# A two-block transformer kernel: projections tied to scores, value halves side by side, differential output by query blocks without normalising, and scaling and gate products on ScalarE and GpSimd

## The chip, the cores and the metric

One core of a Trainium2 chip. TensorE (PE in the profile) multiplies, VectorE (DVE) and ScalarE (ACT) do elementwise work and empty PSUM, GpSimd (POOL) does elementwise work from SBUF, and SyncE (SP) and ScalarE issue DMAs. Each engine runs its own instructions in order. The metric is the device time of the one launch, in microseconds (us).

## The reference

512 tokens of width 1024, float32, pass through two blocks. Cut to what bears on the change:

```python
# block 1
h = rms_norm(x) * (1 + scale) + shift          # shift, scale, gate = silu(c) @ w_ada + b_ada
oa = forgetting_attention(qa, ka, va, fa)      # 8 heads of 64, causal: softmax(qk/8 + c_q - c_k) @ v
ob = sliding_window_sink_attention(qb, kb, vb) # 8 heads of 64 on 2 key heads, window 128, with a sink
y = concat(oa * silu(za), ob * silu(zb)) @ w_out
x = x + gate * rms_norm(y)
# block 2: h @ w_in feeds a convolution, a differential attention and a cross attention
p = softmax(q k / 8 + alibi, causal)           # 8 heads, 2 maps each, q and k normalised
o = (p[0] - lam * p[1]) @ v                    # 128 columns a head
o = rms_norm(o) * subln * 0.8 * silu(gate)
y = g0 * y_conv + g1 * (o @ w_diff) + g2 * y_mem
x = x + y @ w_out2
```

## The kernel before, in words

Every large product is made in three passes: an operand is split into a high part in the fp32r format and the low rest (`wh`, `wl`, `hh`, `hl`), and high*high, high*low and low*high are summed in PSUM. A projection of 128 output rows is 24 matmuls of 512 columns (`mm_T`, L194, matmuls at L198; `mm_W`, L209, at L215; `mm_N`, L203, at L207). `load_w` (L159) brings weights by DMA, splits them on ACT (L170) and on DVE or POOL (L172).

The attentions run item by item (`staged`, L287): an item's scores, an older item's product with the values, a younger item's transposes, and then `fill`, which takes the next steps from a queue of generators (`Fill`, L59), the projections that later work needs. So projections stand between the attention's small matmuls. Below that, a scheduler in the framework sets each engine's final order from the program and from its own estimates, so that projections may move ahead of scores.

Block 1: the sliding-window attention (`swa_sc`, L674; `swa_tp`, L701; `swa_pv`, L716) has 8 items of 4 heads, the forgetting ("fox") attention (`fox_sc`, L758; `causal_tp`, L778; `fox_pv`, L795) 32 items, of 4 query blocks in each of 8 heads. An item makes scores into one of two PSUM banks (tag `sc`, L150); a DVE instruction adds the mask and takes the minimum (L690, L771), ACT takes the exponential and its sum (L692, L773), DVE divides by it (L698, L775), PE transposes (L710, L784), ACT and DVE split the result (L712 and L713, L786 and L787), and PE multiplies with the values in three passes of 64 output rows (L727, L807). Meanwhile `gate_row` (L743) makes the gate of 1024 numbers in 8 pieces: a piece of `w_ada` by DMA, 8 multiply-adds of 128 columns on DVE (`gemv`, L331), a sum over partitions on PE (L751). Splitting `oz` (L832, L833) and the output projection follow.

Block 2: the differential attention (`diff_pro`, L1012; `diff_sc`, L1036; `diff_pv`, L1060) has 32 items of two score maps. DVE normalises both maps and joins them (L1050 to L1053). The product with the values is made once a head, transposed: 128 value columns as weights, queries streaming, three passes (L1077). ACT squares it (L1080), PE sums the squares over partitions (`rsum`, L240), `rsqrt_small` (L223) makes the reciprocal root, DVE makes four diagonal blocks of it (`rdiag`, L248, at L252), PE spreads them (`rbc`, L255, at L258), and `diff_out` (L1088) and `spill` (L959) scale, gate, split and store. The convolution is 31 multiply-adds for each of 8 channel blocks on DVE, at low priority (L933). The cross attention, the gates and the last projections follow.

Of the kernel before, what the change touches and what calls it, by code (L numbers as in the profile page):

```python
# [20 lines left out]
P = 128  # L21
# [71 lines left out]
def two_block_kernel(ctx: ExitStack, tc: tile.TileContext, A: dict, out: bass.AP):  # L93
# [98 lines left out]
    ends = []  # L192
# [30 lines left out]
    def rsqrt_small(wk, ss, n, inv, eps, tag, bufs=None):  # L223
# [4 lines left out]
        dve.tensor_scalar(out=v, in0=ss, scalar1=inv, scalar2=eps, op0=ALU.mult, op1=ALU.add)  # L228
# [113 lines left out]
    with ExitStack() as st:  # L342
# [145 lines left out]
        with low(-ROTP):  # L488
# [4 lines left out]
            dve.tensor_scalar(out=sub8, in0=V("subln"), scalar1=0.8, scalar2=None, op0=ALU.mult)  # L493
# [40 lines left out]
    def va_gen(pools):  # L534
        w = w1n("va")
        parts = [[pl_.tile([P, NT, CW], F32R, tag=f"v{x}{i}", name=f"v{x}") for x in "hl"] for i, pl_ in enumerate(pools)]
        for tp in range(2):
            banks = [mm_tile() for t in range(2)]
            yield from mm_W(banks, w, hh, hl, (2 * tp, 2 * tp + 1))
            for t in range(2):  # L540
                for i, (vh, vl) in enumerate(parts):
                    src = banks[t][:, i * CW:(i + 1) * CW]
                    act.copy(out=vh[:, 2 * tp + t, :], in_=src)
                    dve.tensor_tensor(out=vl[:, 2 * tp + t, :], in0=src, in1=f(vh[:, 2 * tp + t, :]), op=ALU.subtract)  # L544
# [28 lines left out]
    with ExitStack() as stS:  # L573
# [4 lines left out]
        vbh = sw.tile([P, NT, 128], F32R, name="vbh")  # L578
        vbl = sw.tile([P, NT, 128], F32R, name="vbl")
# [94 lines left out]
        def swa_sc(it):  # L674
# [41 lines left out]
        def swa_pv(it):  # L716
# [26 lines left out]
    def gate_row():  # L743
        for j in range(8):
# [3 lines left out]
            acc = gemv(wk, gemv_load(wk, A["w_gate"][j], 128), 128)  # L748
# [9 lines left out]
    def fox_sc(it):  # L758
# [10 lines left out]
        pe.matmul(out=ps[:, :w], lhsT=q2[:, n * P:w], rhs=k2[:, :w], start=False, stop=True)  # L769
# [5 lines left out]
        dve.tensor_scalar(out=p_[:, :w], in0=p_[:, :w], scalar1=st_[:, 2, n:n + 1], scalar2=None, op0=ALU.mult)  # L775
# [19 lines left out]
    def fox_pv(it):  # L795
# [5 lines left out]
        vh, vl = FD["v"][pr // 2]  # L801
        c0 = (2 * (pr % 2) + m) * 64
        pv = pv_tile()
        for j in range(NT):
            a, b = vh[:, j, c0:c0 + 64], vl[:, j, c0:c0 + 64]
            for i, (l_, r_) in enumerate(((a, pth), (a, ptl), (b, pth))):
                pe.matmul(out=pv[0:64, j * P:], lhsT=l_, rhs=r_[:, j, j * P:], start=(j == 0 and i == 0), stop=(j == NT - 1 and i == 2))  # L807
# [3 lines left out]
        act.copy(out=tm[halves(m)[0]], in_=pv[0:64])  # L811
# [9 lines left out]
    fill.until("qk3")  # L821

# [77 lines left out]
    with ExitStack() as st:  # L900
        wk = open_pool(st, "wk2", 2, reuse_waits="tile")
        dp = open_pool(st, "dp", 2, reuse_waits="tile")
        cm_[0] = open_pool(st, "cm2", 1, reuse_waits="tile")
# [55 lines left out]
        def spill(o, z, hd_, ld_, i):  # L959
            a = wk.tile([P, S], F32R, tag="sph", name="sph", bufs=1)  # L960
            b = wk.tile([P, S], F32R, tag="spl", name="spl", bufs=1)
            dve.scalar_tensor_tensor(out=o, in0=z, scalar=0.5, in1=o, op0=ALU.mult, op1=ALU.mult)
            act.copy(out=a, in_=o)
            dve.tensor_tensor(out=b, in0=o, in1=f(a), op=ALU.subtract)
# [47 lines left out]
        def diff_pro(h):  # L1012
# [463 lines left out]
```

## Time and profile before

| | us |
|---|---|
| median of 3 runs (lowest, highest) | 1195.79 (1192.65, 1197.33) |
| profiled execution, its own time | 1195.91 |
| profiled execution, its span | 1194.1 |
| PE busy | 1146.4 (96%), 5584 matmuls |
| DVE busy | 910.0 (76%) |
| ACT busy | 551.1 (46%) |
| POOL busy | 206.4 (17%) |

A matmul's busy time runs from its start to the modelled end of its pipeline and overlaps the next one's, so the busy share of PE hides gaps of some tenths of a microsecond. The distance from one start to the next tells what a matmul takes in a stream. The granted clock is given as a share of full speed, 2.4 GHz; 0.5 is the lower level, 1.2 GHz.

### The profile page before, as it was taken

What the parts mean: (1) busy time and instruction counts of PE and PEld (TensorE: products, weight loads), DVE (VectorE), ACT (ScalarE), POOL (GpSimd) and SP (SyncE); (2) the same over time, 40 slices, a digit from 0 to 9 for tenths busy, and PEclk for the clock granted to TensorE, in tenths of its full rate; (3) what the DMA queues carried; (4) which work ended last, traced back from release to release, by engine and by line L of the source; (5) the groups of instructions that cost most, each with busy time, mean ns of one, the idle gap of its engine ahead of it and who ended that gap; (6) DMA issues with size and microseconds to landing.
All of it is one profiled execution on the core that took longest, in us unless ns stands there. A gap on an engine that the chain in (4) does not pass through costs nothing.

```text
span 1194.1 us, 16211 instructions
## 1 busy us (share of the span) xinstructions
PE 1146.4 (96%) x5584; PEld 940.9 (79%) x5584; DVE 910.0 (76%) x2004; ACT 551.1 (46%) x1157; POOL 206.4 (17%) x158
## 2 busy tenths in 40 slices
PE   7979999897988999999999999999999999999998
PEld 4667888685776888888887888888888888888887
DVE  5877575789867599999999999999793478454342
ACT  5545565554754444554443643355432245242231
POOL 0644100000012202012020121022010131111100
PEclk9989999897999999999999999999999999999999
DMA  9673321254155323333332443243345855422233
GB/s 366 247 249 130 118 89 37 100 180 128 54 187 201 106 86 100 106 102 107 92 106 90 141 142 109 104 131 134 124 148 198 315 173 197 141 96 98 90 106 106
DMA packets 59873, 165.25 MB, mean 138 GB/s; under 512 B 7088, under 2 KB 11440, under 8 KB 58768
## 3 DMA queue, kind: packets, MB, share of 16 engines
q1 hardware_dynamic: 35824, 122.41, 30.9%
q10 hardware_dynamic: 23968, 41.82, 9.9%
q8 instruction: 44, 0.72, 0.2%
q14 instruction: 37, 0.30, 0.1%
HBM read 136.80 MB, written 20.58 MB: 132 GB/s over the span
## 4 chain that ended last, share of the span: by engine, by line
PE 70%; DVE 21%; DMA 4%; issue 3%; ACT 2%; POOL 0%; SPq 0%; ACTq 0%; DVEq 0%
PE mm L198 42%; PE mm L215 13%; DVE cv L933 5%; DVE wl L172 2%; PE mm L207 2%; PE mm L421 2%; DVE acc L337 2%; PE pv L807 1%; DVE dp L1046 1%; DVE ptl L787 1%; PE pv L727 1%; DMA raw<-in_w_out_dram 1%; PE sc L1187 1%; PE pv L1230 1%; PE tp L284 1%
## 5 line engine op out<-in xcount | busy, mean ns | idle before, releaser
L170 ACT CAST wh<-raw 128x512 fp32r<-128x512 f32 (+1 forms) x360 | 214.2, 616 | 205.6 <-PE mm L198 107.1
L172 POOL TENSOR_TENSOR wl<-raw,wh 128x512 fp32r<-128x512 f32 (+1 forms) x94 | 136.2, 1450 | 872.3 <-ACT wh L170 809.1
L172 DVE TENSOR_TENSOR wl<-raw,wh 128x512 fp32r<-128x512 f32 (+1 forms) x266 | 188.5, 720 | 88.2 <-ACT wh L170 87.6
L198 PE MATMUL mm<-hh,wh 128*128 128x512 f32 x640 | 251.7, 393 | 0.0
L198 PE MATMUL mm<-hh,wl 128*128 128x512 f32 x640 | 251.0, 392 | 0.0
L198 PE MATMUL mm<-hl,wh 128*128 128x512 f32 x640 | 250.8, 392 | 0.0
L933 DVE SCALAR_TENSOR_TENSOR cv<-u,vec,cv 128x512 f32<-128x512 f32 x240 | 193.1, 805 | 1.9
L198 PEld LDWEIGHTS mm<-hh,wl 128*128 128x128 f32 x640 | 120.3, 188 | 24.3
L198 PEld LDWEIGHTS mm<-hh,wh 128*128 128x128 f32 x640 | 120.3, 188 | 23.7
L198 PEld LDWEIGHTS mm<-hl,wh 128*128 128x128 f32 x640 | 120.3, 188 | 23.5
L215 PE MATMUL mm<-wh,hh 128*128 128x512 f32 x256 | 101.1, 400 | 2.9 <-DVE vl L544 1.7
L215 PE MATMUL mm<-wh,hl 128*128 128x512 f32 x256 | 101.3, 398 | 1.0 <-DVE hl L858 1.0
L215 PE MATMUL mm<-wl,hh 128*128 128x512 f32 x256 | 101.5, 397 | 0.1
L198 PE MATMUL mm<-bh,wh 128*128 128x512 f32 x192 | 75.2, 392 | 0.0
L198 PE MATMUL mm<-bh,wl 128*128 128x512 f32 x192 | 74.7, 389 | 0.0
L198 PE MATMUL mm<-bl,wh 128*128 128x512 f32 x192 | 74.7, 389 | 0.0
L1048 ACT ACTIVATE dp<-dp,dst 128x128 f32<-128x128 f32 (+3 forms) x64 | 35.9, 561 | 78.3 <-DVE dst L1046 74.5
L215 PEld LDWEIGHTS mm<-wh,hh 128*128 128x128 f32 x256 | 48.7, 190 | 13.8 <-DVE vl L544 2.5
L215 PEld LDWEIGHTS mm<-wh,hl 128*128 128x128 f32 x256 | 48.4, 189 | 10.7 <-DVE hl L858 1.4
L215 PEld LDWEIGHTS mm<-wl,hh 128*128 128x128 f32 x256 | 48.7, 190 | 10.0 <-DVE wl L172 0.5
L207 PE MATMUL mm<-wh,hh 128*128 128x256 f32 (+1 forms) x160 | 47.2, 297 | 1.2 <-ACT hh L449 1.0
L207 PE MATMUL mm<-wl,hh 128*128 128x256 f32 (+1 forms) x160 | 46.9, 295 | 0.0
(330 smaller groups left out, 2120.1 us busy)
## 6 DMA issues: line engine op xcount, KB each, us to landing
raw<-in_w_dram SPq DMA_DIRECT2D x88, 512.0 KB
raw<-in_w_out_dram SPq DMA_DIRECT2D x24, 512.0 KB
raw<-in_w2n_dram SPq DMA_DIRECT2D x24, 512.0 KB
ada<-in_w_ada_dram SPq DMA_DIRECT2D x8, 1024.0 KB
rawm<-in_w_mem_dram SPq DMA_DIRECT2D x8, 512.0 KB
raw<-in_w_mem_dram SPq DMA_DIRECT2D x8, 512.0 KB
raw<-in_w1n_dram SPq DMA_DIRECT2D x8, 512.0 KB
ada<-in_w_gate_dram SPq DMA_DIRECT2D x8, 512.0 KB
```

Of the source, the lines that this page charges most:

```text
L170: act.copy(out=wh, in_=raw[:, s])
L172: eng.tensor_tensor(out=wl, in0=raw[:, s], in1=f(wh), op=ALU.subtract)
L198: m = pe.matmul(out=ps, lhsT=a[:, c0:c0 + P], rhs=at(b, k), start=(n == 0 and i == 0), stop=(n == KT - 1 and i == 2))
L207: pe.matmul(out=ps, lhsT=at(a, k)[:, t * P:(t + 1) * P], rhs=b[:, 0:n], start=(start and m == 0 and i == 0), stop=(stop and m == len(order ...
L215: pe.matmul(out=ps, lhsT=at(a, k)[:, t * P:(t + 1) * P], rhs=b[:, 0:n], start=(m == 0 and i == 0), stop=(m == KT - 1 and i == 2))
L284: pe.transpose(out=ps[:, t * P:(t + 1) * P], in_=src[:, t, c0:c0 + P], identity=ident)
L337: dve.scalar_tensor_tensor(out=d[k % 2], in0=a[:, k, :], scalar=cs[:, k:k + 1], in1=d[k % 2], op0=ALU.mult, op1=ALU.add)
L421: m = pe.matmul(out=banks[t], lhsT=mT[:, k, t * P:(t + 1) * P], rhs=raws[c][k // 2][:, k % 2, :], start=(k == 0), stop=(k == KT - 1))
L727: pe.matmul(out=pv4[0:64], lhsT=l_, rhs=r_[:, j], start=(cnt == 0), stop=(cnt == 3 * nk - 1))
L787: dve.tensor_tensor(out=ptl[:, 0:n + 1, n * P:w], in0=tv, in1=f(pth[:, 0:n + 1, n * P:w]), op=ALU.subtract)
L933: dve.scalar_tensor_tensor(out=a, in0=u[:, j:j + S], scalar=dw[:, m * 31 + j:m * 31 + j + 1], in1=a, op0=ALU.mult, op1=ALU.add)
L1048: act.activation(out=p_[:, :w], in_=p_[:, :w], func=AF.Exp, scale=-1.0, bias=st_[:, 0, n, m:m + 1], accum_out=st_[:, 1, n, m:m + 1])
```

## The change

- **Tied projections.** `swa_sc` and `fox_sc` keep their newest score matmul in `anchor`, and `mm_T` and `mm_W` order their matmuls behind it (`tie`), in PE's order alone. After the fox attention the anchor is cleared.
- **Values side by side.** High and low values of a key block stand in one tile (`vb`, `vv`, `dvv`). In `swa_pv` and `fox_pv` they are the weights together, 64 + 64 columns: two matmuls take the place of three, the two halves of the output are added by ACT's copy and a new DVE addition.
- **Differential output by query blocks.** The product with the values is made in each of the 32 items, with the transposed map as weights and 256 columns of values streaming (high and low), and a second matmul of 128 columns for the low map. The two softmax divisions become one factor, lam * s0 / s1, and the epsilon is scaled by s0 squared. The output has tokens on partitions: ACT sums squares, POOL multiplies by the reciprocal root (`diff_norm`), PE transposes it (`transposed`), and `spill` reads it from PSUM. `rsum`, `rdiag` and `rbc` go from this stage. The pool of the transposed maps has two buffers, of a quarter of the size.
- **Scaling and gate products.** The fox division goes from DVE to ACT. In `gate_row` POOL multiplies the whole piece, 128x1024, and DVE adds it up in three steps.

```diff
+    ends, anchor = [], [None]
+    def tie(m):
+        if anchor[0] is not None:
+            after(m, anchor[0])
     def mm_T(ps, w, c0, xh, xl, order=range(KT)):
...
+                if n in (0, 4) and i == 0:
+                    tie(m)
...
     def mm_W(banks, w, xh, xl, ts, order=range(KT), n=NW):
...
+                    if m % 2 == 0 and i == 0:
+                        tie(x)
...
     def swa_pv(it):
...
-                a, b = vbh[:, j0 + j, 64 * g:64 * g + 64], vbl[:, j0 + j, 64 * g:64 * g + 64]
-                for l_, r_ in ((a, ph), (a, pl), (b, ph)):
-                    pe.matmul(out=pv4[0:64], lhsT=l_, rhs=r_[:, j], start=(cnt == 0), stop=(cnt == 3 * nk - 1))
+                for r_ in (ph, pl):
+                    pe.matmul(out=pv4, lhsT=vb[:, j0 + j, g].rearrange("p a d -> p (a d)"), rhs=r_[:, j], start=(cnt == 0), stop=(cnt == 2 * nk - 1))
...
-            act.copy(out=tm[0:64], in_=pv4[0:64, 0::2, :])
-            act.copy(out=tm[64:128], in_=pv4[0:64, 1::2, :])
+            for m in range(2):
+                a, b = halves(m)
+                act.copy(out=tm[a], in_=pv4[b, m::2, :])
+                dve.tensor_tensor(out=tm[a], in0=pv4[a, m::2, :], in1=tm[a], op=ALU.add)
...
     def gate_row():
...
-            acc = gemv(wk, gemv_load(wk, A["w_gate"][j], 128), 128)
+            a = gemv_load(wk, A["w_gate"][j], 128)
+            pool.tensor_tensor(out=a, in0=a, in1=cs.unsqueeze(2).to_broadcast([P, KT, 128]), op=ALU.mult)
+            yield
+            for n in (4, 2, 1):
+                dve.tensor_tensor(out=a[:, 0:n, :], in0=a[:, 0:n, :], in1=a[:, n:2 * n, :], op=ALU.add)
+            acc = a[:, 0, :]
...
     def fox_sc(it):
...
-        dve.tensor_scalar(out=p_[:, :w], in0=p_[:, :w], scalar1=st_[:, 2, n:n + 1], scalar2=None, op0=ALU.mult)
+        act.activation(out=p_[:, :w], in_=p_[:, :w], func=AF.Copy, scale=st_[:, 2, n:n + 1])
...
     def fox_pv(it):
...
-            for i, (l_, r_) in enumerate(((a, pth), (a, ptl), (b, pth))):
-                pe.matmul(out=pv[0:64, j * P:], lhsT=l_, rhs=r_[:, j, j * P:], start=(j == 0 and i == 0), stop=(j == NT - 1 and i == 2))
+            for i, r_ in enumerate((pth, ptl)):
+                pe.matmul(out=pv[:, j * P:], lhsT=vv[:, j, 2 * (pr % 2) + m].rearrange("p a d -> p (a d)"), rhs=r_[:, j, j * P:], start=(j == 0 and i == 0), stop=(j == NT - 1 and i == 1))
...
-        act.copy(out=tm[halves(m)[0]], in_=pv[0:64])
+        act.copy(out=tm[a], in_=pv[b])
+        dve.tensor_tensor(out=tm[a], in0=pv[a], in1=tm[a], op=ALU.add)
...
     def diff_sc(it):
...
-            dve.reciprocal(out=rr[:, n, :], in_=st_[:, 1, n, :])
-            dve.tensor_tensor(out=rr[:, n, 1:2], in0=rr[:, n, 1:2], in1=nlam, op=ALU.mult)
-            dve.tensor_scalar(out=pms[1][:, :w], in0=pms[1][:, :w], scalar1=rr[:, n, 1:2], scalar2=None, op0=ALU.mult)
-            dve.scalar_tensor_tensor(out=pms[0][:, :w], in0=pms[0][:, :w], scalar=rr[:, n, 0:1], in1=pms[1][:, :w], op0=ALU.mult, op1=ALU.add)
+            dve.reciprocal(out=rr[:, n:n + 1], in_=st_[:, 1, n, 1:2])
+            dve.scalar_tensor_tensor(out=rr[:, n:n + 1], in0=rr[:, n:n + 1], scalar=nlam, in1=st_[:, 1, n, 0:1], op0=ALU.mult, op1=ALU.mult)
+            dve.scalar_tensor_tensor(out=pms[0][:, :w], in0=pms[1][:, :w], scalar=rr[:, n:n + 1], in1=pms[0][:, :w], op0=ALU.mult, op1=ALU.add)
...
     def diff_pv(it):
...
+            for j in range(n + 1):
+                v = vv[:, j, h % 2]
+                pe.matmul(out=pv[:, 0:256], lhsT=pth[:, j, :], rhs=v.rearrange("p a d -> p (a d)"), start=(j == 0), stop=False)
+                pe.matmul(out=pv[:, 0:P], lhsT=ptl[:, j, :], rhs=v[:, 0, :], start=False, stop=(j == n))
+            act.copy(out=o[:, n, :], in_=pv[:, P:256])
+            dve.tensor_tensor(out=o[:, n, :], in0=pv[:, 0:P], in1=o[:, n, :], op=ALU.add)
+            q = wk.tile([P, P], F32, tag="doq", name="doq", bufs=2)
+            act.activation(out=q, in_=o[:, n, :], func=AF.Square, accum_out=ss[:, n:n + 1])
...
+        def diff_norm(h):
...
+            r = rsqrt_small(wk, ss, NT, 1.0 / 128, ev, "or")
+            pool.tensor_tensor(out=o, in0=o, in1=r.unsqueeze(2).to_broadcast([P, NT, P]), op=ALU.mult)
         def diff_out(h):
-            o = D.pop(("o", h))
-            r = rbc(D.pop(("dg", h)))
-            dve.scalar_tensor_tensor(out=o, in0=o, scalar=sub8, in1=r, op0=ALU.mult, op1=ALU.mult)
+            o, _ = D.pop(("o", h))
+            ps = transposed(o, 0)
             fill.until(("dg", h // 2))
-            spill(o, D["dg", h // 2, h % 2], odh_d, odl_d, h)
+            spill(ps, sub8, D["dg", h // 2, h % 2], odh_d, odl_d, h)
```

How the orders move is shown at three places. PE where the sliding-window attention ends and the fox attention starts, before (`sc` are scores, `tp` transposes, `pv` products with values, `mm` projections):

```order
L688 MATMUL sc<-kb_1205,qs 128x256
L689 MATMUL sc<-kbl_1206,qs 128x256
L768 MATMUL sc<-k_1590,qs 128x128
L769 MATMUL sc<-k_1592,q_1591 128x128
L768 MATMUL sc<-k_1590,qs 128x256
L769 MATMUL sc<-k_1592,q_1591 128x256
L710 MATMUL tp<-cst,spt 128x128 x8
L727 MATMUL pv<-sph,vbh 64x512
L727 MATMUL pv<-spl,vbh 64x512
L727 MATMUL pv<-sph,vbl 64x512
```

and in the changed kernel:

```order
L699 MATMUL sc<-kb_1204,qs 128x256
L700 MATMUL sc<-kbl_1205,qs 128x256
L786 MATMUL sc<-k_1590,qs 128x128
L787 MATMUL sc<-k_1592,q_1591 128x128
L221 MATMUL mm<-wh,hh 128x512
L221 MATMUL mm<-wl,hh 128x512
L221 MATMUL mm<-wh,hl 128x512
L786 MATMUL sc<-k_1590,qs 128x256
L787 MATMUL sc<-k_1592,q_1591 128x256
L722 MATMUL tp<-cst,spt 128x128 x8
L738 MATMUL pv<-sph,vb 128x512
L738 MATMUL pv<-spl,vb 128x512
```

Twelve `mm` matmuls stand between the first two fox scores (three of them are shown), where there were none. From the first sliding-window score to the first fox score there were 228 projection matmuls and are 168; from there to the last fox product there were 219 and are 291; before both there were 276 and are 264.

DVE at the start of the fox attention, in the changed kernel (L789 and its second row are the mask and minimum of an item, L792 the reciprocal, L765 the sums of a gate piece, L805 the low part of a transposed map):

```order
L789 ISA fp,fst<-sc,cst 128x384
L789 ISA fst 128x1
L792 RECIPROCAL fst<-fst 128x1 x2
L765 TENSOR_TENSOR ada<-ada 128x512
L765 TENSOR_TENSOR ada<-ada 128x256
L765 TENSOR_TENSOR ada<-ada 128x128
L789 ISA fp,fst<-sc,cst 128x512
L805 TENSOR_TENSOR ptl<-tp,pth 128x128
```

and a stretch of the fox attention before:

```order
L771 ISA fp,fst<-sc,cst 128x512
L771 ISA fst 128x1
L335 TENSOR_SCALAR acc<-ada,cs 128x128 x2
L337 SCALAR_TENSOR_TENSOR acc<-ada,cs,acc 128x128
L787 TENSOR_TENSOR ptl<-tp,pth 128x128
L774 RECIPROCAL fst<-fst 128x1
L787 TENSOR_TENSOR ptl<-tp,pth 128x2x128
L338 TENSOR_TENSOR acc<-acc 128x128
L775 TENSOR_SCALAR fp<-fp,fst 128x384
```

Three sums after a product on POOL stand where nine small instructions a piece did, and the fourth item's minimum stands behind the first piece's sums.

PE in the fox attention of the changed kernel, the second and third head (all rows from one projection to the next, repeats left out):

```order
L802 MATMUL tp<-cst,fp 128x128 x7
L823 MATMUL pv<-pth,vv 128x512
L769 MATMUL tp<-ada,cst 128x128
L786 MATMUL sc<-k_2461,qs 128x128
L787 MATMUL sc<-k_2463,q_2462 128x128
L786 MATMUL sc<-k_2461,qs 128x256
L823 MATMUL pv<-ptl,vv 128x512
L786 MATMUL sc<-k_2461,qs 128x512
L786 MATMUL sc<-k_2470,qs 128x128
L802 MATMUL tp<-cst,fp 128x128
L786 MATMUL sc<-k_2470,qs 128x256
L786 MATMUL sc<-k_2470,qs 128x512
```

Eight items' scores follow one another here without a projection.

## Rows read from the trace of the kernel before

**Rows 1.** Stages: us, busy us (instructions) of PE, PEld, DVE, ACT, POOL, PEclk, DMA share, GB/s

```profile
139.00:212.00 73.00, 72.61 (x370) 59.49 (x370) 47.37 (x148) 42.48 (x117) 5.28 (x4) 1.00 0.21 66
212.00:250.00 38.00, 33.87 (x147) 25.42 (x146) 31.34 (x96) 22.58 (x57) 4.02 (x3) 0.87 0.44 144
250.00:275.00 25.00, 25.00 (x133) 20.71 (x132) 20.16 (x63) 13.26 (x30) 1.29 (x1) 1.00 0.50 147
275.00:300.00 25.00, 16.82 (x66) 10.66 (x65) 23.57 (x86) 12.11 (x32) 1.72 (x1) 0.73 0.40 122
300.00:335.60 35.60, 30.33 (x167) 22.65 (x166) 27.44 (x80) 22.50 (x55) 1.42 (x1) 1.00 0.17 53
...
426.50:761.00 334.50, 328.59 (x1761) 281.37 (x1760) 327.43 (x758) 157.65 (x349) 54.34 (x33) 0.99 0.34 109
761.00:1194.00 433.00, 428.32 (x1975) 356.04 (x1973) 268.54 (x416) 158.59 (x294) 64.80 (x43) 1.00 0.42 144
```

**Rows 2.** Chain that ended last: start us, us, work; two streams of projections

```profile
399.96 11.28 PE mm L207 x94
...
726.09 10.24 PE mm L198 x45
```

**Rows 3.** Timeline of PE, a differential product: start us, busy us, work

```profile
744.56 0.34 PE L1077 MATMUL pv<-pth,dvh 128*128 128x384 f32 x1
744.74 0.34 PE L1077 MATMUL pv<-ptl,dvh 128*128 128x384 f32 x1
...
745.62 0.27 PE L1077 MATMUL pv<-pth,dvl 128*128 128x128 f32 x1
745.73 0.45 PE L198 MATMUL mm<-hl,wh 128*128 128x512 f32 x1
```

**Rows 4.** Timeline of PE, a fox product, with 64 weight columns

```profile
320.72 0.22 PE L807 MATMUL pv<-pth,vh 128*64 128x128 f32 x1
320.78 0.22 PE L807 MATMUL pv<-ptl,vh 128*64 128x128 f32 x1
```

**Rows 5.** Waits from 196 to 340: who waited for whom, us in total, times, longest

```profile
PEld sc L768 <- DVE fst L771: 7.3, 11, 3.0
```

**Rows 6.** DVE by line, 212 to 336: count | busy us, mean ns | idle before

```profile
L337 DVE SCALAR_TENSOR_TENSOR acc<-ada,cs,acc 128x128 f32<-128x128 f32 x48 | 16.7, 370 | 0.1
L771 DVE CUSTOM_DVE_ANT_0 fp<-sc,cst 128x128 f32<-128x128 f32 (+3 forms) x32 | 15.1, 484 | 4.0 <-PE tp L784 3.9
L787 DVE TENSOR_TENSOR ptl<-tp,pth 128x128 fp32r<-128x128 f32 (+3 forms) x32 | 15.0, 484 | 2.4 <-ACT pth L786 2.3
L775 DVE TENSOR_SCALAR fp<-fp,fst 128x128 f32<-128x128 f32 (+3 forms) x32 | 12.0, 382 | 0.4
L335 DVE TENSOR_SCALAR acc<-ada,cs 128x128 f32<-128x128 f32 x16 | 5.6, 363 | 1.9 <-DMA ada<-in_w_gate_dram 1.9
```

**Rows 7.** One line's instructions, the convolution's norm and a normalising product: ns min/median/max

```profile
L1284 DVE TENSOR_TENSOR raw<-raw,lnm x4: 694/1778/1793, 961.0 to 965.0; 128x512 f32<-128x512 f32 x4
L1284 POOL TENSOR_TENSOR raw<-raw,lnm x4: 1732/1742/1806, 961.0 to 966.2; 128x512 f32<-128x512 f32 x4
...
L987 POOL TENSOR_TENSOR xqn<-xqn,ry x4: 1895/1896/2343, 698.4 to 804.2; 128x1024 f32<-128x1024 f32 x4
```

**Rows 8.** ACT by line, 212 to 336

```profile
L773 ACT ACTIVATE fp<-fp,fst 128x128 f32<-128x128 f32 (+3 forms) x32 | 18.0, 563 | 8.9 <-DVE fst L771 7.9 <-DVE fst L774 0.4
L786 ACT CAST pth<-tp 128x128 fp32r<-128x128 f32 (+3 forms) x32 | 13.1, 425 | 11.5 <-PE tp L784 6.3 <-DMA gb<-in_rows_dram 3.1 <-DVE ggb L753 1.9
L773 ACT ACTIVATION_READ_ACCUMULATOR fp<-fp,fst 128x1 f32 x32 | 6.1, 189 | 0.0
```

**Rows 9.** Chain that ended last, a load of a gate piece

```profile
265.02 4.02 DMA ada<-in_w_gate_dram
```

**Rows 10.** DVE by line in the differential attention, 426.5 to 761

```profile
L1052 DVE TENSOR_SCALAR dp<-dp,drr 128x128 f32<-128x128 f32 (+3 forms) x32 | 17.3, 539 | 0.1
L252 DVE TENSOR_SCALAR rdiag<-cst,ry 128x128 f32<-128x128 f32 x28 | 8.8, 377 | 0.0
```

**Rows 11.** Timeline of PE in the differential attention: a wait for the diagonal blocks

```profile
548.40 0.46 PE L258 MATMUL tp<-rdiag,cst 128*128 128x128 f32 x2 [1.50 <-DVE rdiag L252]
549.53 0.94 PE L258 MATMUL tp<-rdiag,cst 128*128 128x128 f32 x6 [0.67 <-DVE rdiag L252]
```

More of the change, by code (lines that the diff above doesn't have):

```diff
@@ L214, in mm_W @@
                 for i, (a, b) in enumerate(((xh, wh), (xh, wl), (xl, wh))):
-                    pe.matmul(out=ps, lhsT=at(a, k)[:, t * P:(t + 1) * P], rhs=b[:, 0:n], start=(m == 0 and i == 0), stop=(m == KT - 1 and i == 2))
+                    x = pe.matmul(out=ps, lhsT=at(a, k)[:, t * P:(t + 1) * P], rhs=b[:, 0:n], start=(m == 0 and i == 0), stop=(m == KT - 1 and i == 2))
+                    if m % 2 == 0 and i == 0:
+                        tie(x)
             if m % 2 and m < KT - 1:
@@ L535, in va_gen @@
         w = w1n("va")
-        parts = [[pl_.tile([P, NT, CW], F32R, tag=f"v{x}{i}", name=f"v{x}") for x in "hl"] for i, pl_ in enumerate(pools)]
+        parts = [pl_.tile([P, NT, 4, 2, 64], F32R, tag=f"vv{i}", name="vv") for i, pl_ in enumerate(pools)]
         for tp in range(2):
@@ L540, in va_gen @@
             for t in range(2):
[L541 to L544, printed above, removed]
+                for i, vv in enumerate(parts):
+                    src = banks[t][:, i * CW:(i + 1) * CW].rearrange("p (h d) -> p h d", d=64)
+                    act.copy(out=vv[:, 2 * tp + t, :, 0, :], in_=src)
+                    dve.tensor_tensor(out=vv[:, 2 * tp + t, :, 1, :], in0=src, in1=f(vv[:, 2 * tp + t, :, 0, :]), op=ALU.subtract)
             yield
@@ L768, in fox_sc @@
         pe.matmul(out=ps[:, :w], lhsT=q1[:, n * P:w], rhs=k1[:, :w], start=True, stop=False)
-        pe.matmul(out=ps[:, :w], lhsT=q2[:, n * P:w], rhs=k2[:, :w], start=False, stop=True)
+        anchor[0] = pe.matmul(out=ps[:, :w], lhsT=q2[:, n * P:w], rhs=k2[:, :w], start=False, stop=True)
         p_ = wk.tile([P, S], F32, tag="fp", name="fp", bufs=4)
@@ L810, in fox_pv @@
         tm = fxd["tm"]
-        act.copy(out=tm[halves(m)[0]], in_=pv[0:64])
+        a, b = halves(m)
+        act.copy(out=tm[a], in_=pv[b])
+        dve.tensor_tensor(out=tm[a], in0=pv[a], in1=tm[a], op=ALU.add)
         if m == 1:
@@ L902, in two_block_kernel @@
         dp = open_pool(st, "dp", 2, reuse_waits="tile")
[L903 removed]
+        cm_[0] = open_pool(st, "cm2", 2, reuse_waits="tile")
         D = {}
@@ L1074, in diff_pv @@
-            for j in range(NT):
-                a, b = vh[:, j, c0:c0 + P], vl[:, j, c0:c0 + P]
-                for i, (l_, r_) in enumerate(((a, pth), (a, ptl), (b, pth))):
-                    pe.matmul(out=pv[:, j * P:], lhsT=l_, rhs=r_[:, j, j * P:], start=(j == 0 and i == 0), stop=(j == NT - 1 and i == 2))
-            o = wk.tile([P, S], F32, tag="do", name="do", bufs=3)
-            q = wk.tile([P, S], F32, tag="doq", name="doq", bufs=1)
-            act.activation(out=q, in_=pv, func=AF.Square)
@@ L1081, in diff_pv @@
-            act.copy(out=o, in_=pv)
-            fill(1)
-            if h == 7:
-                D["ss", h] = rsum(q)
-            D["oq", h] = q
-            D["o", h] = o
+            pth, ptl = D.pop(("dpt", h, n))
+            vv = D["dv", h // 2]
+            if n == 0:
+                D["o", h] = (wk.tile([P, NT, P], F32, tag="do", name="do", bufs=3), wk.tile([P, NT], F32, tag="oss", name="oss"))
+            o, ss = D["o", h]
+            pv = pv_tile()
+            for j in range(n + 1):
+                v = vv[:, j, h % 2]
+                pe.matmul(out=pv[:, 0:256], lhsT=pth[:, j, :], rhs=v.rearrange("p a d -> p (a d)"), start=(j == 0), stop=False)
+                pe.matmul(out=pv[:, 0:P], lhsT=ptl[:, j, :], rhs=v[:, 0, :], start=False, stop=(j == n))
```

83 lines of the change are left out of this document (45 added, 38 removed).

## The prediction

> **What bounds the kernel now.** I read the windows by stage first, to find where TensorE (PE) has room, then the chain of waits, then PE's timeline for what a matmul takes in a stream, and last the lines and waits of the one stage that loses time.
>
> The chain gives the measure: 45 projection matmuls of 512 columns take 10.24 us, 0.227 each, and 94 of 256 columns 11.28 us, 0.12 each [rows 2]. From one start to the next a matmul of 384 columns takes 0.18, one of 128 columns 0.11 with 128 weight columns [rows 3] and 0.06 with 64 [rows 4]. With these prices a stage's matmuls can be laid end to end and compared with its length. The projections of the late block fill PE: after 761 us it is busy 428 of 433 us at full clock [rows 1], so freeing another engine there brings nothing. The sliding-window stage, 139 to 212, is busy 72.6 of 73 us [rows 1]; by start distances some 2 us are lost.
>
> The exception is 212 to 335.6 us, where the sliding-window attention ends and the fox attention runs: 123.6 us. Its matmuls are 219 projections (49.7), 32 pairs of scores (10.2), 96 transposes (10.6), 16 matmuls of gate sums (1.8), 96 fox products (14.1), 13 late sliding-window products (3.0): about 89. So **34 us are holes**. The reader is to see in the windows that 25 of these microseconds, 275 to 300, have only 66 matmuls, a granted clock of 0.73 and DVE busy 23.57 of 25 [rows 1]: no projections are left there. In the waits, scores stand 7.3 us behind DVE's minimum, which frees the score bank [rows 5]. DVE's lines show what fills it: 64 multiply-adds of the gate (16.7 + 5.6), the minimum 15.1, the low parts 15.0, the division 12.0 [rows 6].
>
> In the differential attention, 426.5 to 761, DVE is busy 327.4 of 334.5 us [rows 1], but much of that is convolution, which may wait. PE's start distances lose some 14 us there; waits for diagonal blocks of 1.50 and 0.67 us are a part [rows 11].
>
> **The change part by part.**
>
> *Matmuls.* Sliding window: three products become two, 14 fewer of 0.227: −3.2. Fox, a head: three times (0.227 + 0.18 + 0.12 + 0.06) = 1.76 becomes twice (0.227 + 0.18 + 0.12 + 0.11) = 1.27, since 128 weight columns take the last one from 0.06 to 0.11: −3.9 for 8 heads. Differential, a head: three times 0.637 = 1.91 becomes 10 key blocks of 0.12 + 0.11 = 2.3: +3.1 for 8. Squares' sums and spreads, 32 matmuls each, go (−7.0), 32 transposes of 0.11 come (+3.5). Sum **−7.5**, all of it on PE's full stream or in a stage that PE paces.
>
> *Tie, sliding window.* By the listing 60 projections leave this stage (228 to 168), and 72 join the fox stage. Moved work costs nothing by itself, 0.227 where it goes as where it comes from. The sliding-window items keep 24 projections each, 5.4 us; with two score banks an item's later scores wait for DVE. Bounds: 0, and one wait such as the longest of [rows 5], 3.0, for each of 8 items, 24. The present stage loses 2 with as many banks; I take 5: **+3**.
>
> *Fox, DVE.* It loses the division, 12.0, and the multiply-adds, 22.3 [rows 6]. It gains three sums for each of 8 pieces: 0.69 for 512 columns free, 1.78 against POOL [rows 7], 0.37 for 128 by the nearest row [rows 6], some 0.5 between: 12.4 free, 21 locked; I take 13, since each sum follows its own product and only the next piece's can meet it. It gains 8 additions of the output halves, 0.69 each, 5.5. Net −16. What this uncovers is ACT: 32 scalings of 128 to 512 columns; between the cast, 0.425, and the exponential, 0.563 [rows 8], I take 0.46: +15.
>
> *Fox, holes.* The stage's matmuls grow to 89 + 16.3 (72 projections) − 3.9 − 1 = 101 and so cover more, but in the changed listing 20 of 32 items still stand in runs without a projection. There ACT needs 0.563 + 0.189 + 0.425 [rows 8] + 0.46 = 1.64 an item, PE about 0.9: 20 × 0.74 = 15. Besides, the items' minimum is queued on DVE behind a piece's sums, which wait for its load, 4.0 [rows 9], and POOL's product, 1.9 [rows 7]; scores, ACT and PE wait for that minimum. Most pieces are covered by projections; I count half of one at the start, 3, and one in the last bare run, 6. Holes 15 + 9 = 24 instead of 34: **−10**. Bounds: 8 (a few bare items) and 62 (below).
>
> Here a rule speaks against the change. A plain DVE addition took 694 ns at best and 1778 in the median beside a POOL product of 1742 [rows 7]. The Trainium skill, "SBUF — State Buffer", section "Who interferes with whom", says that a DVE instruction with two SBUF inputs contends with a GpSimd instruction that reads SBUF, and that the other waits for the whole instruction. The trace agrees with it in those rows. By the rule as the only guide the eight products would cost DVE some 15 us and the first rival would be the forecast; by the minimum and the low part, which each read PSUM and whose means of 484 ns [rows 6] show no such meeting, the sum stays.
>
> *Differential.* DVE loses 32 scalings of the second map, 17.3, and the diagonal blocks, 32 × 0.377 = 12 [rows 10], and 8 scalings of the output, 8 × 0.69 = 5.5 by [rows 7]; it gains 32 additions of 128 columns, 12 at the price of the diagonal blocks: −23 of 327. Convolution fills that. What PE sees is that the waits of [rows 11] go; in their place each item's product waits for the copy and addition of the one before to leave the single value bank, with a whole item of other matmuls between. Bounds −14 and +15 (below); **−4**, holes 14 to 10. What DVE saves beyond is convolution done earlier, and behind 761 us PE's stream is full: nothing.
>
> **Sum.** −7.5 + 3 − 10 − 4 = −18.5 against the profiled execution's 1195.9, which is 0.1 from the median: **1177**. Its own range is 1166 to 1184.
>
> **The rivals.**
>
> *The holes stay (0.23).* POOL's eight products, 8 × 1.9 = 15, hold DVE's two-input instructions for as long as DVE was relieved (16), and ACT is the new pace: fox holes stay 34. For it: DVE's 1778 beside POOL [rows 7]. Against: the minimum and the low part read PSUM. −7.5 + 3 − 4 = −8.5: 1187.
>
> *The holes nearly go (0.14).* The 72 added projections stand between items so well that 8 us of holes are left and the clock never falls; ties cost nothing, differential −6: −7.5 − 26 − 6 = −39.5, 1156. For it: 300 to 335.6 us, where projections were interleaved, ran at clock 1.00 [rows 1]. Against: the runs of eight items in the listing.
>
> *Slower: gate pieces hold DVE (0.12).* One mechanism: the minimum is queued behind sums that wait for load and product, 8 × (4.0 + 1.9) = 47 us, none covered, beside the 15 of bare items: 62 of holes, +28. −7.5 + 3 + 28 − 4 = +19.5, 1215. It decides once fox holes pass 34 + 8.5 = 42.5. For it: DVE already idled 1.9 for a piece's load [rows 6]. Against: the pieces have two buffers, and that 1.9 was all of it in the whole stage.
>
> *No net effect, by the value bank (0.09).* The differential products use the bank 32 times instead of 8; if each of 24 further uses holds PE for the copy and addition, 0.425 + 0.37 = 0.8, that is +19 on the −4: −7.5 + 3 − 10 + 15 = 0, 1196.
>
> That the change does not do what it says is excluded by the listings: projections did move.
>
> **How the numbers follow.** Forecast 0.42, rivals as above. A measurement of this kernel can tell about 0.5%, 6 us. Faster (below 1190): all of the forecast, 0.18 of the first rival, 0.14 of the second, 0.74. Within: 0.05 of the first and the value bank, 0.14. Slower 0.12. The range 1152 to 1196 holds the forecast, the first rival, most of the second and half of the value bank: 0.42 + 0.23 + 0.11 + 0.05 = 0.81.
>
> **What would show it.** Right: some 60 us from the first sliding-window score to the first fox score, then about 125 to the last fox product, with start distances that lose 24; no stretch of 25 us in the fox stage at clock 0.73; ACT's low wait for DVE's minimum replaced by ACT busy; no wait on diagonal blocks. Wrong: sums of a gate piece with DVE idle behind POOL or a load for 3 us or more and scores waiting behind them (the slower rival); a sliding-window stage over 65; product matmuls of the differential stage waiting for DVE's addition of the item before.

## The result and the profile after

The changed kernel takes 1207.98 us (median of 4 runs, 1205.66 to 1208.73); the kernel before, measured beside it, 1195.47. The ratio is 1.0094, 95% interval 1.0070 to 1.0117: slower by 0.9%, some 12 us. Forecast were 1177 us and a range of 1152 to 1196.

The head of the profile of the changed kernel:

```profile
span 1203.9 us, 16139 instructions
...
PE 1140.9 (95%) x5506; PEld 939.9 (78%) x5506; DVE 903.6 (75%) x1916; ACT 572.9 (48%) x1269; POOL 229.0 (19%) x174
```

PE has 78 matmul records less and DVE is busy 6 us less, and yet the span is 10 us longer: the time is in gaps. The windows by stage show where (columns as in [rows 1]):

```profile
139.00:200.00 61.00, 57.78 (x297) 47.59 (x297) 52.22 (x158) 42.44 (x120) 5.15 (x4) 1.00 0.23 74
200.00:250.00 50.00, 45.18 (x203) 36.98 (x204) 29.37 (x81) 26.62 (x65) 6.54 (x4) 0.90 0.24 81
250.00:275.00 25.00, 22.04 (x96) 17.47 (x95) 15.36 (x42) 14.95 (x36) 5.06 (x3) 0.86 0.41 118
275.00:291.90 16.90, 15.40 (x75) 12.75 (x74) 14.63 (x33) 8.55 (x20) 3.60 (x2) 1.00 0.51 161
291.90:307.60 15.70, 2.47 (x8) 1.57 (x7) 9.99 (x16) 3.53 (x7) 7.32 (x4) 0.61 0.54 177
307.60:325.00 17.40, 17.31 (x75) 14.21 (x74) 14.05 (x39) 13.49 (x31) 1.52 (x1) 0.76 0.08 22
325.00:348.60 23.60, 17.16 (x91) 12.63 (x89) 15.50 (x45) 17.43 (x46) 0.00 (x0) 1.00 0.20 59
442.00:745.00 303.00, 295.98 (x1607) 251.94 (x1606) 293.60 (x685) 155.61 (x412) 58.77 (x38) 0.99 0.34 109
745.00:1203.00 458.00, 455.22 (x2098) 378.50 (x2097) 292.26 (x457) 168.47 (x311) 67.97 (x46) 1.00 0.42 143
```

The row 291.9 to 307.6 is new: in 15.7 us PE has 8 matmuls, DVE, the busiest engine, works 9.99, and the clock falls to 0.61. In the next row PE is busy throughout, but at 0.76. Against [rows 1] the late stages are sound: behind 745 PE's stream is full, as it was.

I laid each stage's matmuls end to end with the prices of [rows 2] to [rows 4], every record counted, and took what is left of the stage as holes, for all kernels alike; these are estimates. Matmul work falls from 1106 to 1091 us. Holes rise from 78 to 103:

| a stage, from the end of the one above | us before, after | holes before, after |
|---|---|---|
| from the first matmul to the first sliding-window score | 133.0, 132.4 | 19.8, 21.9 |
| to the first fox score | 73.2, 61.9 | 2.0, 6.6 |
| to the last fox product | 120.8, 146.5 | 32.3, 46.6 |
| to the first differential score | 93.4, 95.6 | 9.2, 11.4 |
| to the last differential product | 319.1, 301.4 | 12.2, 15.2 |
| to the last matmul | 444.5, 456.3 | 2.6, 1.2 |

The fox stage takes 14 of the 25 us. The first stage, which the change hardly touches, lasts 129.6 to 136.0 us in the single profiled runs of all kernels below, so times are compared by medians and places by profiles.

### The profile page after: what moved, and what is told of

Same layout as the page of the kernel before. It is cut to its first block, busy times and chain, and to the rows that moved or that the text cites. A ratio compares the mean times of both kernels' runs of the same rounds, so it can differ in the third digit from the quotient of the medians.

```text
span 1203.9 us, 16139 instructions
## 1 busy us (share of the span) xinstructions
PE 1140.9 (95%) x5506; PEld 939.9 (78%) x5506; DVE 903.6 (75%) x1916; ACT 572.9 (48%) x1269; POOL 229.0 (19%) x174
## 4 chain that ended last, share of the span: by engine, by line
PE 72%; DVE 18%; DMA 3%; ACT 3%; issue 2%; POOL 1%; SPq 0%; ACTq 0%; DVEq 0%; POOLq 0%
PE mm L202 42%; PE mm L221 16%; DVE cv L952 3%; PE mm L213 3%; DVE wl L172 2%; PE mm L432 2%; DVE acc L348 1%; PE tp L295 1%; DMA raw<-in_w2n_dram 1%; PE sc L1216 1%; PE pv L1259 1%; DVE dp L1064 1%; DVE ada L765 1%; DMA ada<-in_w_ada_dram 1%; PE pv L823 1%
## 5 line engine op out<-in xcount | busy, mean ns | idle before, releaser
L172 POOL TENSOR_TENSOR wl<-raw,wh 128x512 fp32r<-128x512 f32 (+1 forms) x94 | 134.3, 1430 | 788.6 <-ACT wh L170 743.6
L172 DVE TENSOR_TENSOR wl<-raw,wh 128x512 fp32r<-128x512 f32 (+1 forms) x266 | 196.4, 751 | 97.8 <-ACT wh L170 97.0
```

Of the source, the lines that this page charges most:

```text
L172: eng.tensor_tensor(out=wl, in0=raw[:, s], in1=f(wh), op=ALU.subtract)
```

## The wait behind the new hole

PE's timeline around the hole (L787 is a fox score, L769 a gate sum over partitions):

```profile
291.68 0.39 PE L786 MATMUL sc<-k,qs 128*128 128x512 f32 x1
291.91 0.39 PE L787 MATMUL sc<-k,q 68*128 68x512 f32 x1
299.14 0.77 PE L769 MATMUL tp<-ada,cst 128*128 128x128 f32 x2 [6.84 <-DVE ada L765]
302.09 0.77 PE L769 MATMUL tp<-ada,cst 128*128 128x128 f32 x2 [2.19 <-DVE ada L765]
307.06 0.77 PE L769 MATMUL tp<-ada,cst 128*128 128x128 f32 x2 [4.21 <-DVE ada L765]
```

Three gate sums stand next to one another on PE, with nothing between them to do. The chain that ended last says what each waits for:

```profile
289.12 3.71 DMA ada<-in_w_gate_dram
...
293.00 1.87 POOL ada L762
...
294.90 1.75 DVE ada L765
...
296.67 2.01 DVE ada L765
...
298.70 0.30 DVE ada L765
...
299.14 0.78 PE tp L769 x2
...
299.94 3.44 DMA ada<-in_w_gate_dram
...
303.51 1.90 POOL ada L762
...
305.44 0.70 DVE ada L765
...
307.06 0.78 PE tp L769 x2
```

A load, POOL's product, DVE's three sums, PE's sum, and at 299.94, as that ends, the next load. The piece's tile has two buffers. Before, DVE's multiply-adds wrote accumulators of their own, and a load buffer was free once DVE had read it. Now the sums are made in place, PE reads the result out of the load tile itself (its first 128 columns), and the load of the piece after next waits for PE.

DVE's first two sums took 1.75 and 2.01 us there. POOL's timeline beside them:

```profile
292.97 1.90 POOL L762 TENSOR_TENSOR ada<-ada,cs 128x1024 f32<-128x1024 f32 x1 [11.83 <-DMA ada<-in_w_gate_dram]
294.82 1.26 POOL L172 TENSOR_TENSOR wl<-raw,wh 128x512 fp32r<-128x512 f32 x1
296.04 2.35 POOL L762 TENSOR_TENSOR ada<-ada,cs 128x1024 f32<-128x1024 f32 x1
```

The first sum ends half a microsecond after POOL's split of a weight (L172), the second 0.3 us after POOL's next product. Elsewhere in this stage such sums took 0.67 and 0.41; the hold costs 1.1 + 1.6 = 2.7 us in the middle of the chain. (This is the meeting of [rows 7]. By the rule of the Trainium skill named in the prediction, "SBUF — State Buffer", section "Who interferes with whom", DVE additions with two SBUF inputs contend with POOL instructions that read SBUF. The trace agrees: 1.75 and 2.01 us beside POOL, 0.67 and 0.41 without it.)

## The experiments

The experiments were timed in four sets, e1 to e4, e5 to e8, e9 to e12 and e13 to e15, each in five rounds beside the kernel before, whose medians were 1196.0, 1196.4, 1197.0 and 1197.5 us; the ratios are to it. The changed kernel was timed by itself beside 1195.5. Kernels of one set are compared by their times, kernels of different sets by their ratios, where 0.001 is 1.2 us.

| kernel | us | ratio, 95% interval |
|---|---|---|
| changed | 1208.0 | 1.0094 [1.0070, 1.0117] |
| e1, own tile for the last sum | 1203.3 | 1.0057 [1.0037, 1.0076] |
| e2, gate on DVE | 1195.7 | 0.9993 [0.9980, 1.0006] |
| e3, no tie | 1200.4 | 1.0041 [1.0026, 1.0056] |
| e4, division on DVE | 1201.8 | 1.0045 [1.0029, 1.0061] |
| e5, differential part alone | 1189.4 | 0.9937 [0.9916, 0.9958] |
| e6, gate on DVE, no tie | 1199.4 | 1.0016 [0.9996, 1.0036] |
| e7, gate and division on DVE | 1194.6 | 0.9978 [0.9961, 0.9994] |
| e8, e7 without the tie | 1196.6 | 0.9998 [0.9981, 1.0014] |
| e9, differential part and tie | 1186.6 | 0.9918 [0.9898, 0.9938] |
| e10, values side by side alone | 1202.7 | 1.0051 [1.0033, 1.0069] |
| e11, e8 with a third fox pass | 1199.0 | 1.0018 [1.0003, 1.0033] |
| e12, e8 without the additions | 1190.5 | 0.9944 [0.9925, 0.9962] |
| e13, e1 with the product on DVE | 1200.6 | 1.0024 [1.0010, 1.0039] |
| e14, e9 and division on ACT | 1185.1 | 0.9893 [0.9873, 0.9912] |
| e15, e9 and gate on POOL, own tile | 1189.4 | 0.9934 [0.9915, 0.9954] |

**The gate: e1, e2, e13.**

```diff
# e1
-            for n in (4, 2, 1):
+            for n in (4, 2):
                 dve.tensor_tensor(out=a[:, 0:n, :], in0=a[:, 0:n, :], in1=a[:, n:2 * n, :], op=ALU.add)
-            acc = a[:, 0, :]
+            acc = wk.tile([P, 128], F32, tag="acc0", name="acc")
+            dve.tensor_tensor(out=acc, in0=a[:, 0, :], in1=a[:, 1, :], op=ALU.add)
# e2: product, sums and one yield go
+            acc = gemv(wk, gemv_load(wk, A["w_gate"][j], 128), 128)
# e13: as e1, and
-            pool.tensor_tensor(out=a, in0=a, in1=cs.unsqueeze(2).to_broadcast([P, KT, 128]), op=ALU.mult)
+            dve.tensor_tensor(out=a, in0=a, in1=cs.unsqueeze(2).to_broadcast([P, KT, 128]), op=ALU.mult)
```

> Changed kernel, but the last of the three sums of a gate piece goes to a tile of its own (128 columns), so that the piece's load buffer is free after DVE and not only after PE's sum over partitions. Buffer theory: the loads of pieces 6, 7 and 8 start well before PE's sum of the piece two before, the three waits of 7.0, 2.5 and 4.5 us in front of PE's gate sums mostly go, fox holes fall from 47 to 33-39 us, time 1194 to 1200. Rival, POOL's product and the tree as such hold DVE: waits of the same size stay in front of the gate sums, 1204 to 1209. Rival, bare runs set the end: the waits go but come back as scores waiting for DVE or ACT, 1203 to 1208.

> Changed kernel, but the gate pieces are multiplied and added on DVE as in the kernel before (64 multiply-adds of 128 columns, no product on POOL, own accumulators, one step less a piece); all else changed. Buffer theory: as with the own tile, 1194 to 1201, not better than it since DVE has 9 us more. Rival, POOL's product and the tree hold DVE: clearly better than the own tile, 1192 to 1198, with the own tile at 1204 to 1209. Rival, bare runs: no gain or slower, 1206 to 1212, as DVE is fuller.

> Run with the own tile for a piece's last sum, and the product of 128x1024 on DVE instead of POOL: eight products and their sums on DVE, some 8 x (1.3 + 1.3) = 21 us there against the 28 of 64 multiply-adds, nothing on POOL. Theory that what was left of the gate's cost beside the buffer (1203.3 against 1195.7) is POOL's 1.9 us between load and sums and the DVE instructions that it holds: 1195 to 1199. Rival, the rest came from another order (a key copy that a score waits 4.3 us for) and from the one long instruction in DVE's queue: 1201 to 1205.

e1 gives back 4.4 of 11 us by the ratios, less than the buffer theory said, and ends at the foot of the bare-run rival's range. The waits in front of the gate sums are gone from its profile, but in the same region a score now waits 4.3 us for a copied key:

```profile
277.73 0.39 PE L770 MATMUL tp<-acc,cst 128*128 128x128 f32 x2
282.40 0.30 PE L787 MATMUL sc<-k,qs 128*128 128x128 f32 x1 [4.29 <-DMA k<-k]
```

So the late buffer made the three waits, and without them PE is held by what was next. That much the rival had right; it named DVE and ACT, and the longest wait is for a DMA. The own tile has two buffers as well, and a load still comes behind a sum on PE, four pieces back in place of two: in e1's trace the loads of the last four pieces start at 252.47, 260.93, 275.21 and 278.99, each 1 to 3 us behind the start of PE's sum of the piece four before, at 250.66, 258.65, 272.48 and 277.73. The gate on DVE (e2) is 7.6 us better still, although DVE does more. With the product on DVE (e13) about half of these are got back, 3.9 us by the ratios, between the ranges of its two theories. The hold of 2.7 us in the chain above would be a part of that; as the intervals of e1 and e13 touch, its size is not shown. The product itself is shorter on DVE; the tile's summary in e13, ahead of that of the changed kernel:

```profile
L762 DVE TENSOR_TENSOR ada<-ada,cs x8: 1205/1222/1226, 218.1 to 289.1; 128x1024 f32<-128x1024 f32 x8
```

```profile
L762 POOL TENSOR_TENSOR ada<-ada,cs x8: 1895/1897/2347, 214.1 to 303.5; 128x1024 f32<-128x1024 f32 x8
```

The last 3.7 us between e13 and e2 are not settled: their orders differ in the whole fox stage, and e2 has one step less a piece in the queue.

**The tie and the division: e3, e4, e6, e7.** e3 and e6 take the tie away, with the gate on POOL and on DVE; e4 and e7 put the division back on DVE:

```diff
# e3, e6
     def tie(m):
-        if anchor[0] is not None:
-            after(m, anchor[0])
+        return
# e4, e7; e14 is e9 with these two lines exchanged
-        act.activation(out=p_[:, :w], in_=p_[:, :w], func=AF.Copy, scale=st_[:, 2, n:n + 1])
+        dve.tensor_scalar(out=p_[:, :w], in0=p_[:, :w], scalar1=st_[:, 2, n:n + 1], scalar2=None, op0=ALU.mult)
```

> Changed kernel, but the projections are not tied behind scores. Theory that the tie costs the sliding-window stage its cover (holes 2 to 6.6 us) and gives the fox stage nothing that it can use: sliding-window holes back to 2-3 and fox holes not above 47, 1200 to 1205. Rival, the tie's 72 projections in the fox stage do cover: fox holes rise to 55-70, 1212 to 1225.

> Changed kernel, but the fox division is on DVE again (32 instructions, 12 us) and off ACT (about 15 us). Theory that ACT paces the bare runs of eight items (325 to 345 us): these lose some 0.4 us less an item, fox holes 47 to 40-44, 1201 to 1206. Rival, DVE is still the pace: 1208 to 1214. Buffer theory alone: within 2 us of the changed kernel, 1206 to 1210, the waits for the gate sums stay.

> Changed kernel with the gate on DVE and without the tie. Theory that both lose independently (gate 12 us, tie 7 to 8 us): 1187 to 1190. Rival, the tie only lost because it brought the gate sums into bare runs, so that with the gate on DVE it is worth nothing or helps: 1194 to 1200.

> Changed kernel with the gate and the fox division on DVE, tie kept. Theory that ACT's scaling paces the bare runs whatever the gate does (6 us): 1188 to 1191. Rival, with gate and division DVE is the pace as in the kernel before: 1195 to 1199.

By the ratios the tie's absence gains 6.3 us in the changed kernel and the division's return 5.9. With the gate on DVE the tie's absence costs 2.8 and the division's return gains 1.8, neither more than the intervals leave open. So neither part is shown to lose by itself; a clear loss shows only beside the gate on POOL, and why it is larger there is not shown. The theory of e6, that gate and tie lose independently, fell, and so did that of e7, that ACT's scaling costs its 6 us whatever the gate does. e3 warns against adding up waits: PE has four in front of gate sums, of 3.1 to 3.4 us each, and yet e3 is only 3.0 us slower than e6, which has none of them; there PE stands for other reasons, 7.3 us in seven waits of scores for DVE's minimum.

**The parts alone: e5, e8, e9, e10.** e5 is the kernel before with the change's functions from `dv_gen` to `diff_out` and what they call, as in the diff ahead; e10 the kernel before with `va_gen`, `swa_pv`, `fox_pv` and their tiles as changed; e8 has both; e9 is e5 with the tie. Against the changed kernel e5 undoes, beside the gate, the division and the tie,

```diff
# e5, and e9 without the last two lines; fox_pv, and swa_pv alike
+            a, b = vh[:, j, c0:c0 + 64], vl[:, j, c0:c0 + 64]
-            for i, r_ in enumerate((pth, ptl)):
+            for i, (l_, r_) in enumerate(((a, pth), (a, ptl), (b, pth))):
...
-        act.copy(out=tm[a], in_=pv[b])
-        dve.tensor_tensor(out=tm[a], in0=pv[a], in1=tm[a], op=ALU.add)
+        act.copy(out=tm[halves(m)[0]], in_=pv[0:64])
...
-            after(m, anchor[0])
+            return
```

> Kernel before with the differential part alone (output by query blocks, one factor for both maps, norm on POOL); block 1 as before. By fp32 matmuls counted as two passes each, sums and spreads of squares give 2 x 32 x 2 x 0.11 = 14.1, the products cost 3.1 and the transposes 3.5: matmul work -7.4. Theory that the stage keeps its holes within 2 us: 1188 to 1191. Rival, the value bank and the norm's chain through POOL hold PE by 4 us or more: 1192 to 1197.

> Kernel before with the values side by side in both attentions of block 1 and nothing else: 46 matmuls of block 1 less, 7 us of PE, 24 additions of halves more on DVE (8 x 0.69 + 16 x 0.42 = 12 us). Theory that these stages are paced by DVE and ACT at a clock that falls when PE idles: slower, 1200 to 1206, with the windows of 275 to 350 us at a lower granted clock than the 0.73, 1.00 and 1.00 of the kernel before. Rival, the loss in the run of all three came from elsewhere (an order that shifted): 1190 to 1196.

> Gate and division on DVE, no tie: what is left of the change is the values side by side in block 1 and the differential part. Matmul work -7.1 - 7.4. Theory that the values side by side save their matmul time but for some 3 us of longer ends (an addition more behind the last product): 4 us below the differential part alone, 1183 to 1187. Rival, fox is paced by DVE and ACT, so that fewer matmuls only make holes: the same as the differential part alone or above, 1188 to 1193.

> Kernel before with the differential part and the tie; values apart, gate and division on DVE. With the gate on DVE and the values side by side the tie gained 3.7 us (1199.4 to 1195.7). Theory that it gains this without the values too: 1184 to 1187. Rival, it gains only what the values side by side had opened (bare runs that PE leaves idle), and costs the sliding-window stage its cover: 1189 to 1194.

The differential part gains 0.63%; with the tie (e9) another 2.3 us by the ratios, which the intervals don't separate. The values side by side, 7 us of matmuls less, make the kernel before 0.5% slower, and cost 7.2 us on top of e5 (e8). Windows of 275 to 350 us of e5,

```profile
275.00:300.00 25.00, 16.82 (x67) 11.16 (x66) 23.79 (x87) 12.53 (x33) 1.81 (x1) 0.73 0.44 137
300.00:325.00 25.00, 23.78 (x130) 18.24 (x129) 21.92 (x68) 17.85 (x47) 1.44 (x1) 1.00 0.21 64
325.00:350.00 25.00, 20.96 (x96) 16.07 (x95) 12.91 (x27) 13.01 (x29) 2.58 (x2) 0.93 0.41 128
```

and of e10:

```profile
275.00:300.00 25.00, 15.50 (x52) 10.88 (x49) 23.48 (x78) 11.31 (x28) 1.65 (x1) 0.60 0.43 122
300.00:325.00 25.00, 23.35 (x113) 18.63 (x114) 22.63 (x69) 16.80 (x44) 1.41 (x1) 0.92 0.21 64
325.00:350.00 25.00, 19.19 (x75) 14.64 (x75) 13.82 (x30) 11.45 (x27) 1.30 (x1) 0.80 0.26 85
```

DVE is busy alike, over nine tenths at first. PE, with fewer matmuls to do, is through no earlier, and its clock is lower in every row.

**What in the values costs: e11, e12.**

```diff
# e11
-            for i, r_ in enumerate((pth, ptl)):
+            for i, r_ in enumerate((pth, ptl, pth)):
# e12, in fox_pv and in swa_pv
-        dve.tensor_tensor(out=tm[a], in0=pv[a], in1=tm[a], op=ALU.add)
```

> The run of all three (values side by side, differential part, gate and division on DVE, no tie) with a third pass of the high part put back into the fox products: 5.1 us of PE work at full clock, no other engine touched; the output adds the high part twice. Theory that PE is not the pace there: not slower by more than 2, 1194 to 1199, the fox stage's holes fall by 4 to 6 us. Rival, PE's work counts: 1200 to 1203.

> The run of all three without the 24 additions of the two output halves on DVE (the half of the low values alone is copied, the high half is left out of the output). Theory that the additions, on a DVE that is busy 9 tenths of the fox stage and behind each last product, cost what the matmuls saved: back to 1186 to 1190. Rival, the saved matmul time turns into holes whatever DVE does: 1193 to 1197.

e12 is back to e5's time: the additions cost some 6 us, and the 7 us of saved matmuls are worth about nothing there (0.9944 without the additions, 0.9937 in e5 with the three passes apart; the intervals leave some 3 us open). e11 costs 2.4 us for 5.1 us of matmuls; the interval of the two ratios leaves 0 to 5 open, so how far PE's work counts is not settled by it. In the changed kernel the additions are these:

```profile
L744 DVE TENSOR_TENSOR stm<-pv,stm 64x256 f32<-64x256 f32 x16 | 6.7, 418 | 2.6 <-ACT stm L743 2.3
L829 DVE TENSOR_TENSOR ftm<-pv,ftm 64x512 f32<-64x512 f32 x8 | 5.5, 688 | 3.0 <-ACT ftm L828 2.9
```

12.2 us of DVE, each behind a copy on ACT and ahead of the release of the one value bank. PE waits for the bank itself only once in this kernel, a product 2.3 us for an addition of L744; in e8 such a wait is 2.4. By which way the rest of the 6 us reaches PE is not shown.

**Without the values: e14, e15.** e14 is e9 with the division on ACT, e15 is e9 with `gate_row` as in e1, POOL's product and the own tile.

> Differential part and tie, values apart, gate on DVE, and the fox division on ACT: 12 us off a DVE that is busy 80 to 90 hundredths of the fox stage. Theory that DVE paces what projections do not cover: 1181 to 1185, fox holes 23 to 17-20. Rival, ACT paces the bare runs and takes it back: 1186 to 1190.

> Differential part and tie, values apart, division on DVE, and the gate's product on POOL with the last sum in a tile of its own. Theory that the buffer was the fault of POOL's gate, and 9 us less on DVE help: 1181 to 1186. Rival, load, product and sums still stand in a row before PE's sum and hold it: 1190 to 1196.

12 us less on DVE bring 3.0 us by the ratios, and 26 us of fox holes become 24, not the 17 to 20 of its theory; the gate on POOL is 1.9 us slower here. The intervals of e9 overlap with both, so neither is separated from nothing. e14, 1185.1, is the fastest kernel of this study, 1.1% under the kernel before; tie and division together are clear of e5. Its windows:

```profile
250.00:275.00 25.00, 22.26 (x102) 17.48 (x101) 20.52 (x75) 13.93 (x33) 1.77 (x1) 0.92 0.46 142
275.00:300.00 25.00, 22.25 (x119) 17.86 (x118) 18.87 (x53) 20.51 (x47) 1.28 (x1) 1.00 0.33 94
300.00:325.00 25.00, 21.62 (x118) 15.53 (x117) 17.20 (x51) 20.00 (x51) 1.29 (x1) 1.00 0.21 64
```

Here the 25 us at 0.73 of [rows 1] are gone, and ACT and DVE share the load. Its fox stage has 24 us of holes, the kernel before 32. Step by step from it to the changed kernel, by the ratios: values 12 us slower (e2), gate on POOL 12 more.

## Why the prediction was wrong, by its own steps

**The bound.** The place was right: the fox stage holds what can be won and lost. "All of it on PE's full stream or in a stage that PE paces" was the first step that failed. It was said of a stage in which the prediction had itself counted 34 us of holes and DVE busy 23.57 of 25 us. There 3.9 us of fox matmuls less bought nothing that shows (e12 against e5), and the additions, of which the sum let 5.5 us vanish in a relief of 21, cost some 6 us of time (e12 against e8). The 16 additions in the sliding-window stage, 6.7 us, were not counted at all; with the values apart its holes are 3.4 us (e9), with them 6.5 (e2).

**Matmul work.** −7.5 was forecast; with the same prices it is −14.7. Squares' sums and spreads were taken as 32 matmuls each. The trace of before has two records for each instruction (32 sums, and 28 spreads in this stretch):

```profile
L258 PE MATMUL tp<-rdiag,cst 128*128 128x128 f32 x56 | 7.9, 281 | 2.8 <-DVE rdiag L252 2.8
...
L243 PE MATMUL tp<-cst,doq 128*128 128x1 f32 x64 | 7.6, 239 | 0.0
```

So they cost twice what was booked, and their going saves 14 us, not 7. These two have plain float32 operands; the transposes, and the products split into high and low parts, have one record an instruction. Smaller is that the shortest fox product, booked at 0.11 with 128 weight columns, takes 0.06 in the first of its two passes in the changed kernel's trace.

**Tie.** +3 for the sliding-window stage; its holes rose by 4.6, of which 1.4 with values apart (e9). Over the whole kernel it is worth about what it costs or a little more (2.3 us, e9 against e5, not separated from nothing).

**Fox, DVE and ACT.** Sizes were near: the sums 15.4 us (13 forecast), the fox additions 5.5, the scaling 17.2 (15). Taking the 12 us of division off DVE is worth about 3 us in e14 against e9, which the intervals do not separate from nothing; DVE's relief did not bring the 10 us of the next term.

**Fox, holes.** 34 to 24 was forecast, 32 to 47 came: the term of −10 measured +14, the largest miss of the sum. The step that failed is "Most pieces are covered by projections; I count half of one at the start, 3, and one in the last bare run, 6". The prediction priced load and product nearly rightly (3.4 to 3.7 and 1.9 us in the trace) but not that the in-place sum ties the next load to PE's sum, nor that three gate sums follow one another on PE. The order can be read in PE's timeline above, a fox score and then three gate sums; the prediction quoted other places of the listing and not this one. The gate is not all of it: with the gate on DVE (e2) there are still 35 us of holes, with the values apart too (e14) 24. So the 24 of the forecast came only in a kernel without the values side by side and without POOL's product, two parts that the sum counted on.

**Differential.** −4.4 was forecast, matmuls included, and −7.0 measured alone (e5), by another sum: holes did not fall (12.2 to 15.2 in the changed kernel), the matmul work fell by 7.4 instead of 0.4. Against the forecast, the matmul work is 7 us too high and the holes 7 us too low; that these offset each other is luck, and 2.6 us of the −7.0 stand in neither. The waits on diagonal blocks went and others came, none long:

```profile
PE tp L1080 <- DVE dp L1070: 2.1, 1, 2.1
PE tp L295 <- POOL do L1117: 1.6, 2, 1.4
PE tp L295 <- DVE u L945: 1.5, 1, 1.5
PE pv L1101 <- DVE do L1104: 1.0, 1, 1.0
```

The last row is the value bank of the fourth rival: one wait of 1 us, not 19 in all.

**The rivals.** The slower one, given 0.12, named the right chain, load, POOL, sums, and by the prediction's own sign, fox holes past 42.5, it was the one that came. It had the wrong victim: the long waits were those of PE's gate sums, while the scores' weight loads waited 6.5 us for DVE's minimum, not longer than the 7.3 of [rows 5]. Its 47 us were too much, since PE did not wait at five of the eight sums; the gate costs 12. The other half of the loss, the values, was no rival at all: it stood in the sum as a gain.

## What to carry to other kernels

Work taken off an engine is worth its time only in the stretches where that engine's own stream is full; price it by stage, and where a stage has holes, price first what the edit adds to the engine that makes them. When a result moves into the tile that a load filled, ask who reads it last: that reader now releases the buffer and so starts the next load. Parts that each lose beside one flaw may show no loss without it, so undo the flaw before judging them.

## What the runs showed of the hardware

After the 15.7 us hole the granted clock did not come back with the work: in 307.6 to 325 us PE was busy 17.31 of 17.40 us and the clock stood at 0.76, a mean of the two levels, 1.2 and 2.4 GHz; from 325 on it was 1.00, though PE was busy for only 17.16 of 23.60. A multiplication of 128x1024 took 1.90 us on POOL and 1.22 on DVE. The sums and spreads of plain float32 operands have two records an instruction in the trace, the gate sums too (16 for 8), and in a stream each takes its 0.11 us from start to start (the median of L243 and of L258 before).
